# Hybrid decoder block on one core: projection and channel-mixing tiles multiplied in two halves of 256 tokens

## The chip, the core and the metric

The kernel runs on one core of one Trainium2 chip, as one program. A core has a matrix engine (TensorE, PE in the rows; its weight loads are listed as PEld), a vector engine (VectorE, DVE), a scalar engine (ScalarE, ACT), a general engine (GpSimd, POOL) and a queue engine (SyncE, SP), each with its own instruction stream, run in order. They wait for each other through semaphores. Data lies in SBUF, matmul results in the 8 banks of PSUM (512 float32 per partition each). The metric is the device time of one execution in microseconds, from runs without the profiler; one further execution is profiled.

## What is computed

One decoder block on 512 tokens of width 1024, all in float32:

```
mod = silu(c) @ w_ada + b_ada;  shift_m, scale_m, gate_m, shift_f, scale_f, gate_f = split(mod, 6)
h = modulate(rms_norm(x, g_pre_mix), shift_m, scale_m);  p = h @ w_in
y_a = rwkv7_mix(token-shifted part of p: r, k, v, decay, rate, gate) @ w_a     # 12 heads of 64
y_b = dilated_attention_mix(q, k, v of p) @ w_b                                # 3 groups of 4 heads
merged = sigmoid(p_ga) * y_a + sigmoid(p_gb) * y_b
x = x + gate_m * rms_norm(merged @ w_out, g_post_mix)
h = modulate(rms_norm(x, g_pre_ffn), shift_f, scale_f);  u, g = split(h @ w_ffn_in, 2)
out = x + gate_f * rms_norm((silu(u) * g) @ w_ffn_out, g_post_ffn)             # width 2816
```

## The kernel before

Every large product is made from three matmuls. A float32 operand is split into a high part, rounded to the type float32r, and a low part, the rest (`split`: ACT copies the high part, line 111, DVE subtracts for the low part, line 112). `mm3` then adds high x high, high x low and low x high into one PSUM bank. All matmuls of the kernel but the transposes are issued on line 108, so a line alone doesn't tell them apart; the tile names do.

A projection tile is 128 output channels by 512 tokens. Its weights, 128 x 1024, come in by one DMA on SP's queue into `raw` (three buffers), and are split into `hi` and `lo` (two buffers each). The moving operands are the normalised tokens: `hh`/`hl` for the input projection (`gemm_in`, 8 blocks of 128 input channels, so 24 matmuls), `zh`/`zl` for the output projection of the RWKV branch (`wa_tile`, 6 blocks, 18 matmuls), `h2h`/`h2l` for the channel mixing (`ffn_mm`, 24 matmuls). Three PSUM banks named `mm` hold these results; ACT and DVE read a bank once its last matmul is done.

The order of work: the normalisation of x with the first six input tiles (a code of its own, lines 340 on), then the RWKV part in two groups of three head pairs, then attention, the branch outputs and their merge, the product with w_out, and the channel mixing (22 pairs of tiles, then the product with w_ffn_out). The first four channel-mixing tiles are already multiplied in two halves of 256 tokens, because the second half of their input comes later.

An RWKV group is a chain through all engines. DVE substitutes the inverses of 32 x 32 blocks in 31 steps (`fP`, `fT`), transposes them into `T1` (line 529; `T` in the rows) and `N` (lines 530 and 531), PE multiplies `T1` with `Sg`, DVE and ACT copy the result to `Q`, PE multiplies `Q` with `N`, and then come 8 steps of a recurrence with small matmuls of 64 columns (`UV`, `H`, `xs`). The other input tiles, the list `SEQ`, are fillers that PE works on between the steps of this chain. Between them stand the key norms (`key_norm`, matmuls of 2 columns on `cs` and `t`, evacuated by DVE into `ssq`), the transposes of v (line 249) and the ada steps of DVE (line 163, `aw`).

A scheduler sets the order on each engine ahead of time. It takes the instructions in the order of the code, moved by priorities that count instructions: a group is issued with the priority of 1665 instructions earlier (`PRI`), the weights of a tile with a high priority, ada steps with 6681 (`APRI`). It keeps a time of its own for each instruction, and puts a filler where the chain is not ready by that time. On the chip an engine runs what stands next and waits for it.

Of the kernel before, what the change touches and what calls it, by code (L numbers as in the profile page):

```python
# [16 lines left out]
DRAM = bass.MemoryType.DRAM  # L17

P = 128
D = 1024  # L20
S = 512
KT = D // P
# [7 lines left out]
NF = DFF // P  # L30
KAPPA = math.exp(-0.5)
# [4 lines left out]
# columns of the packed per-channel vectors  # L36
# [9 lines left out]
# columns of the packed constants  # L46
# [12 lines left out]
# tiles of the packed weights  # L59
# [5 lines left out]
W_FI = 58  # L65
# [4 lines left out]
# order of the projection tiles around the two head groups  # L70
# [14 lines left out]
def block_kernel(ctx, tc, x, vec, cst, cst2, cst3, crow, ada, win0, lora, wts, wa, out):  # L85
# [41 lines left out]
    def mm3(o, wh, wl, ah, al, start, stop):  # L127
        mm(o, wh, ah, start, False)
        mm(o, wh, al, False, False)
        mm(o, wl, ah, False, stop)  # L130

# [44 lines left out]
    # DRAM scratch  # L176
# [28 lines left out]
    def gemm_in(i):  # L205
        wh, wl = weights(i)
        ps = bank("mm")
        for k in range(KT):
            w = slice(k * P, (k + 1) * P)
            mm3(ps, wh[:, w], wl[:, w], hh[:, k, :], hl[:, k, :], k == 0, k == KT - 1)  # L210
        return ps
# [51 lines left out]
    with ExitStack() as ph0:  # L263
# [82 lines left out]
        # LoRA hidden states  # L346
# [46 lines left out]
    def rwkv_group(gi):  # L393
        p0i = gi * GP
        # LoRA up weights: each of w2 and a2 with its high and low parts stacked on partitions
# [18 lines left out]
        for p in range(GP):  # L414
            pi = p0i + p
            cols = slice(p * P, (p + 1) * P)
            sgm = rp.tile([P, 2, NCH, 2 * C], F32, tag="Sg", name=nm("Sg"), bufs=3)
            Sg[p] = sgm
            scr.append(sgm.rearrange("p e c t -> p (e c t)"))
            # decay and in-context learning rate  # L420
            ps = bank(BT[gi][1])
            mm(ps, uw[:, cols], lw_h, True, False)
            mm(ps, uw[lo64, cols], lw_l[lo64], False, True)
            sg = scr[p][:, 0:520]
            sgv = sg.rearrange("p (c t) -> p c t", t=65)
            G.memset(sgv[:, :, 0:1], 0.0)
            A.activation(sgv[:, :, 1:65], ps.rearrange("p (c t) -> p c t", t=64), AF.Sigmoid, bias=vcol(V_W0, pi))
            ps = bank(BT[gi][2])
            mm(ps, ua[:, cols], la_h, True, False)
            mm(ps, ua[hi64, cols], lw_l[hi64], False, True)  # L430
            A.activation(scr[p][:, 1040:1552], ps, AF.Sigmoid, bias=vcol(V_A0, pi))
        for p in range(GP):
# [15 lines left out]
            # normalised key direction  # L448
# [23 lines left out]
            # gram blocks, keys first  # L472
# [21 lines left out]
        for p in range(GP):  # L494
# [6 lines left out]
            # v with tokens on partitions  # L501
# [7 lines left out]
        # inverses of the 32x32 diagonal blocks by substitution, one block per partition  # L509
# [44 lines left out]
        # chunk recurrence, the pairs of the group in step  # L554
# [5 lines left out]
        for c in range(NCH):  # L560
# [32 lines left out]
            if c % 2 == 1:  # L593
# [11 lines left out]
                # centre each head and sum the squares  # L605
# [16 lines left out]
        # group norm over each head, then back to channels on partitions  # L622
# [176 lines left out]
    def wa_tile(ct):  # L799
# [4 lines left out]
        for k in range(6):  # L804
            w = slice(k * P, (k + 1) * P)
            mm3(ps, wh[:, w], wl[:, w], zh[:, k, :], zl[:, k, :], k == 0, k == 5)
# [136 lines left out]
    for i in range(2, NF):  # L943
        pu, pg = bank("mm"), bank("mm")
        ffn_mm(pu, weights(W_FI + 2 * i), slice(0, S))
        ffn_mm(pg, weights(W_FI + 2 * i + 1), slice(0, S))
# [101 lines left out]
```

## Time and profile before

| | us |
|---|---|
| median of 3 runs | 1030.13 |
| lowest and highest run | 1029.17, 1035.16 |
| span of the profiled execution | 1036.7 |
| PE busy in it | 1004.9 |
| DVE busy in it | 580.4 |
| ACT busy in it | 397.2 |

The profiled execution is 6.6 us above the median. A row of the timeline gives the start, the duration, the engine, the line, the operation, output<-inputs with buffer numbers left out, the shape of the weights and of the moving operand, and the count; a bracket at the end is the time that the engine stood still before it, and what ended that. Matmuls overlap: the distance between two starts is what one costs in a stream, and it is shorter than its duration. The granted clock is PE's, as a share of full speed; 0.50 is the lower of its two levels. A float32 matmul (not float32r) takes several passes, so the chip counts more matmuls than the program.

### The profile page before, as it was taken

To read this page: it belongs to the slowest core of one execution; us is meant where nothing else is said; L and a number is where in the kernel's file an instruction comes from. 1 tells how busy PE (TensorE), PEld (TensorE's weight loads), DVE (VectorE), ACT (ScalarE), POOL (GpSimd) and SP (SyncE) were. 2 spreads that over 40 slices of the span, in tenths; PEclk is the share of its full clock that TensorE was granted. 3 is DMA by queue.
4 is the path that set the end of the run, shared out by engine and by line. 5 is a ranking of instruction groups with operands and counts; after the bars stand their busy time and mean duration, and the time that the engine had idled before them with its cause. 6 is when DMAs were issued, how large, how long until landed. Compare 5 with 4: busy or idle time off the path is not lost.

```text
span 1036.7 us, 13831 instructions
## 1 busy us (share of the span) xinstructions
PE 1004.9 (97%) x5468; PEld 787.8 (76%) x5468; DVE 580.4 (56%) x1050; ACT 397.2 (38%) x633; POOL 42.0 (4%) x85
## 2 busy tenths in 40 slices
PE   6999899999999999999999999999999999999997
PEld 4877778766777877677788768888888888888885
DVE  7885999643499984346646576763333333222134
ACT  7667453421366322331265234632323223222122
POOL 0000000100000010001000100010000000000000
PEclk9999999896999988999999999999999999999999
DMA  9743536322233222117525864063342332322322
GB/s 369 267 160 102 183 102 196 110 64 90 65 104 112 92 92 82 32 41 228 176 74 186 322 202 164 2 229 99 98 122 81 102 96 88 102 92 92 101 82 82
DMA packets 47170, 131.73 MB, mean 127 GB/s; under 512 B 11249, under 2 KB 12033, under 8 KB 47106
## 3 DMA queue, kind: packets, MB, share of 16 engines
q1 hardware_dynamic: 27792, 96.74, 28.7%
q10 hardware_dynamic: 13970, 16.27, 4.9%
q0 software_dynamic: 5344, 17.84, 4.8%
q8 instruction: 43, 0.70, 0.3%
q14 instruction: 21, 0.17, 0.1%
HBM read 116.14 MB, written 14.69 MB: 126 GB/s over the span
## 4 chain that ended last, share of the span: by engine, by line
PE 75%; DVE 11%; issue 7%; DMA 5%; ACT 1%; POOL 0%; ACTq 0%; SPq 0%; DVEq 0%; POOLq 0%
PE ps L108 73%; DVE lo L112 2%; DVE fP L521 1%; DVE fT L525 1%; DMA aw<-in_ada_dram 1%; DMA d_ya<-t 1%; DVE Sg L481 1%; DVE aw L163 1%; DMA gb<-d_gate 1%; DMA x<-in_x_dram 1%; DMA k<-d_k 1%; DMA t<-d_gate 1%; ACT xg L485 0%; PE ps L303 0%; PE ps L906 0%
## 5 line engine op out<-in xcount | busy, mean ns | idle before, releaser
L111 ACT CAST hi<-raw 128x1024 fp32r<-128x1024 f32 (+1 forms) x130 | 132.9, 1023 | 382.9 <-PE ps L108 329.3
L112 DVE TENSOR_TENSOR lo<-raw,hi 128x1024 fp32r<-128x1024 f32 (+1 forms) x130 | 154.6, 1190 | 185.5 <-ACT hi L111 179.7
L108 PE MATMUL ps<-hh,lo 128*128 128x512 f32 x432 | 179.1, 415 | 0.2 <-DVE lo L112 0.2
L108 PE MATMUL ps<-hl,hi 128*128 128x512 f32 x432 | 179.1, 415 | 0.0
L108 PE MATMUL ps<-hh,hi 128*128 128x512 f32 x432 | 175.7, 416 | 1.1 <-ACT hi L111 0.7
L108 PE MATMUL ps<-h2h,hi 128*128 128x512 f32 (+1 forms) x352 | 135.2, 386 | 0.7 <-ACT u L936 0.7
L108 PE MATMUL ps<-h2l,hi 128*128 128x512 f32 (+1 forms) x352 | 135.0, 385 | 0.0
L108 PE MATMUL ps<-h2h,lo 128*128 128x512 f32 (+1 forms) x352 | 134.8, 384 | 0.0
L108 PEld LDWEIGHTS ps<-hh,hi 128*128 128x128 f32 x432 | 84.7, 196 | 20.4 <-issue 2.1
L108 PEld LDWEIGHTS ps<-hh,lo 128*128 128x128 f32 x432 | 84.3, 195 | 19.1 <-issue 1.0
L108 PEld LDWEIGHTS ps<-hl,hi 128*128 128x128 f32 x432 | 84.5, 196 | 18.0 <-issue 0.8
L108 PEld LDWEIGHTS ps<-h2h,hi 128*128 128x128 f32 x352 | 65.8, 187 | 16.0 <-ACT u L936 0.9
L108 PEld LDWEIGHTS ps<-h2l,hi 128*128 128x128 f32 x352 | 65.9, 187 | 14.9
L108 PEld LDWEIGHTS ps<-h2h,lo 128*128 128x128 f32 x352 | 65.9, 187 | 14.8
L163 DVE SCALAR_TENSOR_TENSOR aw<-aw,silur 128x1024 f32<-128x1024 f32 x48 | 58.3, 1220 | 7.8 <-DMA aw<-in_ada_dram 7.7
L937 DVE TENSOR_TENSOR u<-u,ps 128x512 f32<-128x512 f32 x22 | 15.0, 687 | 70.2 <-PE ps L108 62.8
L108 PE MATMUL ps<-hi,fh 128*128 128x512 f32 x144 | 45.2, 394 | 0.0
L108 PE MATMUL ps<-hi,fl 128*128 128x512 f32 x144 | 45.2, 394 | 0.0
L108 PE MATMUL ps<-lo,fh 128*128 128x512 f32 x144 | 45.1, 394 | 0.0
L108 PE MATMUL ps<-UV,Sg 128*64 128x64 f32 x384 | 41.1, 247 | 0.0
L108 PEld LDWEIGHTS ps<-UV,Sg 128*64 128x64 f32 x384 | 26.8, 146 | 11.0 <-issue 3.2
L108 PEld LDWEIGHTS ps<-hi,fl 128*128 128x128 f32 x144 | 26.9, 187 | 6.7
(292 smaller groups left out, 1436.2 us busy)
## 6 DMA issues: line engine op xcount, KB each, us to landing
raw<-in_wts_dram SPq DMA_DIRECT2D x124, 512.0 KB, 3.6
aw<-in_ada_dram SPq DMA_DIRECT2D x40, 512.0 KB, 4.0
d_gate<-t POOLq DMA_DIRECT2D x16, 256.0 KB, 3.0
aw<-in_ada_dram POOLq DMA_DIRECT2D x8, 512.0 KB, 4.6
raw<-in_win_dram SPq DMA_DIRECT2D x8, 384.0 KB, 7.1
raw<-in_wa_dram SPq DMA_DIRECT2D x8, 384.0 KB, 3.8
x<-in_x_dram SPq DMA_DIRECT2D x4, 512.0 KB, 5.1
t<-d_gate ACTq DMA_DIRECT2D x8, 256.0 KB, 4.3
```

Source lines behind the costliest of these rows:

```text
L108: return nc.tensor.matmul(o, l, r, start=start, stop=stop)
L111: A.copy(hi, src)
L112: V.tensor_tensor(out=lo, in0=src, in1=r32(hi), op=ALU.subtract)
L163: V.scalar_tensor_tensor(out=aw, in0=aw, scalar=1.0, in1=silur, op0=ALU.mult, op1=ALU.mult, accum_out=modv[:, i:i + 1])
L481: V.tensor_tensor(out=sgm[:, e, c0:c0 + 4, :], in0=pgr[e].rearrange("p (c t) -> p c t", c=4), in1=m_gram[:, None, :].to_broadcast([P, 4, 2 ...
L521: V.tensor_tensor(out=pv, in0=fU[:, t + 1 + a:t + 1 + b, t, None].to_broadcast([P, b - a, m]), in1=fT[:, t, None, 0:m].to_broadcast([P, b ...
L525: V.tensor_tensor(out=rows, in0=rows, in1=pv, op=ALU.add)
L937: V.tensor_tensor(out=u, in0=u, in1=pg, op=ALU.mult)
```

## The change

`gemm_in`, `wa_tile` and the channel mixing from its third pair of tiles on (`i` from 2) go over a tile twice. First all blocks of input channels are multiplied for tokens 0 to 255 into the first half of the bank, then again for tokens 256 to 511 into the second half. Each weight block is thus loaded twice, and each matmul of 512 columns becomes two of 256. The program has 4576 matmuls before and 6832 after. The loads of weights, the splits, the banks and what reads them are the same, and SP's queue issues the same loads in the same order. In the channel mixing both tiles' weights are now asked for before the first tile's matmuls. The rest of the difference between the files is comments taken out, which moves the lines by one (up to line 205: `mm` stands on line 109) or more.

```diff
+HALVES = (slice(0, S // 2), slice(S // 2, S))
 ...
 def gemm_in(i):
     wh, wl = weights(i)
     ps = bank("mm")
-    for k in range(KT):
-        w = slice(k * P, (k + 1) * P)
-        mm3(ps, wh[:, w], wl[:, w], hh[:, k, :], hl[:, k, :], k == 0, k == KT - 1)
+    for t in HALVES:
+        for k in range(KT):
+            w = slice(k * P, (k + 1) * P)
+            mm3(ps[:, t], wh[:, w], wl[:, w], hh[:, k, t], hl[:, k, t], k == 0, k == KT - 1)
     return ps
 ...
 # wa_tile
-    for k in range(6):
-        w = slice(k * P, (k + 1) * P)
-        mm3(ps, wh[:, w], wl[:, w], zh[:, k, :], zl[:, k, :], k == 0, k == 5)
+    for t in HALVES:
+        for k in range(6):
+            w = slice(k * P, (k + 1) * P)
+            mm3(ps[:, t], wh[:, w], wl[:, w], zh[:, k, t], zl[:, k, t], k == 0, k == 5)
 ...
 # channel mixing, i from 2
-    ffn_mm(pu, weights(W_FI + 2 * i), slice(0, S))
-    ffn_mm(pg, weights(W_FI + 2 * i + 1), slice(0, S))
+    for ps, w in ((pu, weights(W_FI + 2 * i)), (pg, weights(W_FI + 2 * i + 1))):
+        for t in HALVES:
+            ffn_mm(ps, w, t)
```

The scheduler's order changes with it around the RWKV chain. On PE, where group 0's first inverse blocks are multiplied (`T_195`, output on `ps`), this stood before. The rows on `hh` and `hl` are fillers, the last matmuls of tile `ps_2212` and the first of `ps_2246`, which holds v of head pair 3:

```order
L108 MATMUL ps_2212<-hl,hi_2208 128x512
L108 MATMUL ps_2212<-hh,lo_2209 128x512
L108 MATMUL ps_2246<-hh,hi_2242 128x512
L108 MATMUL ps_2246<-hl,hi_2242 128x512
L108 MATMUL ps_2246<-hh,lo_2243 128x512
L108 MATMUL ps_2246<-hh,hi_2242 128x512
L108 MATMUL ps_1266<-T_195_1258,Sg_873 32x32 x8
L108 MATMUL ps_2246<-hl,hi_2242 128x512
L108 MATMUL ps_2246<-hh,lo_2243 128x512
L108 MATMUL ps_2246<-hh,hi_2242 128x512
L108 MATMUL ps_2246<-hl,hi_2242 128x512
L108 MATMUL ps_1266<-T_195_1258,Sg_873 32x32 x8
```

And now; `ps_2620` is the tile of gate 8, which stands one before v of pair 3 in `SEQ`, and the matmul of 2 columns is a key norm's:

```order
L109 MATMUL ps_2620<-hh,hi_2616 128x256
L109 MATMUL ps_1434<-T_195_1426,Sg_1041 32x32 x8
L109 MATMUL ps_2620<-hl,hi_2616 128x256
L109 MATMUL ps_2620<-hh,lo_2617 128x256
L109 MATMUL ps_2620<-hh,hi_2616 128x256
L109 MATMUL ps_2620<-hl,hi_2616 128x256
L109 MATMUL ps_2589<-cs_67,t_2587 128x2 x4
L109 MATMUL ps_2620<-hh,lo_2617 128x256
L109 MATMUL ps_2620<-hh,hi_2616 128x256
L109 MATMUL ps_2620<-hl,hi_2616 128x256
L109 MATMUL ps_2620<-hh,lo_2617 128x256
L109 MATMUL ps_1434<-T_195_1426,Sg_1041 32x32 x8
```

The first `T_195` matmuls have moved ahead by the columns of 0.90 tile, and ahead of three key norms of four program matmuls each. On DVE, at the same place, the end of the substitution, the transposes and the first copy stood like this (`ssq` evacuates a key norm):

```order
L387 TENSOR_SCALAR ssq_2178<-ps_2181 128x8
L521 TENSOR_TENSOR fP_1136<-fU_1134,fT_1135 128x87
L387 TENSOR_SCALAR ssq_2178<-ps_2189 128x8
L525 TENSOR_TENSOR fT_1135<-fT_1135,fP_1136 128x3x29
L387 TENSOR_SCALAR ssq_2178<-ps_2197 128x8
L521 TENSOR_TENSOR fP_1136<-fU_1134,fT_1135 128x60
L525 TENSOR_TENSOR fT_1135<-fT_1135,fP_1136 128x2x30
L521 TENSOR_TENSOR fP_1136<-fU_1134,fT_1135 128x31
L525 TENSOR_TENSOR fT_1135<-fT_1135,fP_1136 128x31
L529 STREAM_TRANSPOSE T_195_1258<-fT_1135 32x1024 x2
L163 SCALAR_TENSOR_TENSOR aw_2342,modv<-aw_2342,silur 128x1024
L530 STREAM_TRANSPOSE N_1259<-fT_1135 128x1024
```

And now (`lo_2675` is the low part of v of pair 3, which stood 12 rows ahead of the transposes before):

```order
L527 TENSOR_TENSOR fT_1303<-fT_1303,fP_1304 128x3x29
L523 TENSOR_TENSOR fP_1304<-fU_1302,fT_1303 128x60
L527 TENSOR_TENSOR fT_1303<-fT_1303,fP_1304 128x2x30
L523 TENSOR_TENSOR fP_1304<-fU_1302,fT_1303 128x31
L527 TENSOR_TENSOR fT_1303<-fT_1303,fP_1304 128x31
L531 STREAM_TRANSPOSE T_195_1426<-fT_1303 32x1024 x2
L532 STREAM_TRANSPOSE N_1427<-fT_1303 128x1024
L533 STREAM_TRANSPOSE N_1427<-fT_1303 128x1024
L544 COPY Q_1451<-ps_1434 32x256
L113 TENSOR_TENSOR lo_2675<-raw_2672,hi_2674 128x1024
L554 COPY N_1427<-ps_1456 32x32x8
L389 TENSOR_SCALAR ssq_2586<-ps_2589 128x8
```

The key norms, the split and one ada step have moved behind the transposes. On ACT two loads of an activation table, for the key norm's square root and for the sigmoid after it, have moved from ahead of the copy to `Q` into the recurrence's first step. In group 1 the first matmuls on `T_473` stand behind the columns of 40.90 tiles instead of 41.17, and the four transposes of v that stood ahead of them (line 249) now stand behind; the other differences are of a few fillers.

## Rows read from the trace of the kernel before

**Rows 1.** The page: the span, PE's busy time, and the granted clock in 40 slices.

```profile
span 1036.7 us, 13831 instructions
...
PE 1004.9 (97%) x5468; PEld 787.8 (76%) x5468; DVE 580.4 (56%) x1050; ACT 397.2 (38%) x633; POOL 42.0 (4%) x85
...
PEclk9999999896999988999999999999999999999999
```

**Rows 2.** Windows, channel mixing; columns: PE, PEld, DVE, ACT, POOL, clock, DMA, GB/s.

```profile
684.00:906.00 222.00, 222.00 (x954) 178.17 (x953) 82.97 (x97) 62.60 (x80) 3.76 (x7) 1.00 0.36 113
```

**Rows 3.** Timeline of PE, channel mixing: first and last of 53 starts.

```profile
799.73 0.39 PE L108 MATMUL ps<-h2l,hi 128*128 128x512 f32 x1
...
811.86 0.39 PE L108 MATMUL ps<-h2h,lo 128*128 128x512 f32 x1
```

**Rows 4.** Timeline of PE, output projection: first and last of 21 starts.

```profile
596.24 0.40 PE L108 MATMUL ps<-zh,lo 128*128 128x512 f32 x1
...
600.90 0.40 PE L108 MATMUL ps<-zl,hi 128*128 128x512 f32 x1
```

**Rows 5.** Timeline of PE, input projection: first and last of 22 starts.

```profile
479.80 0.39 PE L108 MATMUL ps<-hh,lo 128*128 128x512 f32 x1
...
484.56 0.39 PE L108 MATMUL ps<-hh,lo 128*128 128x512 f32 x1
```

**Rows 6.** Timeline of PE, first channel-mixing tiles in halves: first and last of 20 starts.

```profile
679.27 0.28 PE L108 MATMUL ps<-h2l,hx 128*128 128x256 f32 x1
...
681.42 0.28 PE L108 MATMUL ps<-h2h,lx 128*128 128x256 f32 x1
```

**Rows 7.** Timeline of PE, where these halves begin: first and last of 7 starts.

```profile
655.84 0.28 PE L108 MATMUL ps<-h2h,hi 128*128 128x256 f32 x1
...
656.54 0.28 PE L108 MATMUL ps<-h2h,hi 128*128 128x256 f32 x1
```

**Rows 8.** Timeline of PE, input projection at half clock: first and last of three starts.

```profile
202.41 0.63 PE L108 MATMUL ps<-hh,hi 128*128 128x512 f32 x1
...
203.26 0.63 PE L108 MATMUL ps<-hh,lo 128*128 128x512 f32 x1
```

**Rows 9.** Timeline of DVE around group 0's transposes into T and N.

```profile
178.85 1.22 DVE L112 TENSOR_TENSOR lo<-raw,hi 128x1024 fp32r<-128x1024 f32 x1
...
180.49 0.16 DVE L387 TENSOR_SCALAR ssq<-ps 128x8 f32<-128x8 f32 x1
...
182.84 0.17 DVE L387 TENSOR_SCALAR ssq<-ps 128x8 f32<-128x8 f32 x1 [1.70 <-PE ps L108]
...
183.88 4.02 DVE L529 STREAM_TRANSPOSE T<-fT 32x1024 f32<-32x1024 f32 x2
187.93 1.23 DVE L163 SCALAR_TENSOR_TENSOR aw<-aw,silur 128x1024 f32<-128x1024 f32 x1
...
191.48 0.43 DVE L542 COPY Q<-ps 32x256 f32<-32x256 f32 x1
```

**Rows 10.** Timeline of PE there: the last key norm, what follows it, and T.

```profile
181.85 0.95 PE L108 MATMUL ps<-cs,t 128*128 128x2 f32 x8
182.66 0.48 PE L108 MATMUL ps<-hh,lo 128*128 128x512 f32 x1
...
185.97 1.07 PE L108 MATMUL ps<-T,Sg 32*32 32x32 f32 x16 [0.53 <-DVE T L529]
```

**Rows 11.** Timeline of ACT there: a load of an activation table.

```profile
180.01 1.28 ACT L389 ACT_TABLE_LOAD   x1
```

**Rows 12.** Timeline of PE, group 1: the transposes of v, and T.

```profile
372.59 0.60 PE L249 MATMUL ps<-cs,t 128*128 128x128 f32 x4
374.95 1.07 PE L108 MATMUL ps<-T,Sg 32*32 32x32 f32 x16 [0.83 <-DVE T L529]
```

**Rows 13.** Timeline of PE, before attention: a wait for a DMA.

```profile
487.35 2.22 PE L108 MATMUL ps<-k,q 64*128 64x128 f32 x6 [2.40 <-DMA k<-d_k]
```

**Rows 14.** Windows right behind that wait (columns as in group 2).

```profile
487.60:494.50 6.90, 6.90 (x18) 4.99 (x18) 2.49 (x4) 0.00 (x0) 0.00 (x0) 0.51 0.73 225
```

**Rows 15.** Windows in group 0's recurrence (columns as in group 2).

```profile
211.00:238.00 27.00, 27.00 (x227) 18.41 (x225) 10.62 (x22) 7.43 (x17) 0.00 (x0) 1.00 0.26 79
238.00:255.00 17.00, 17.00 (x84) 11.01 (x84) 6.09 (x12) 4.05 (x9) 0.00 (x0) 0.51 0.19 63
```

**Rows 16.** The core's span and its mean granted clock.

```profile
core 0: 1036.7 us, clock 0.967
```

## The prediction

> **What bounds the kernel now.** I read the page first. TensorE (PE) is busy 1004.9 of 1036.7 us, and its granted clock is at or near full in nearly every slice, with dips in slices 8, 10, 15 and 16 [rows 1]. So the reader should expect the time to be PE's own work plus the few stretches in which PE stands still or runs at half clock; another engine matters only where PE waits for it. The windows show this for the channel mixing: from 684 to 906 us PE is busy 222.00 of 222.00 us at a granted clock of 1.00 [rows 2].
>
> Busy time does not price a matmul, because matmuls overlap: what counts is the distance from start to start, which the timeline gives. In the channel mixing, 52 steps of 512 columns lie between 799.73 and 811.86 us: 12.13 / 52 = 233.3 ns each [rows 3]. In the RWKV branch's output projection, 20 steps take 4.66 us, 233.0 ns [rows 4]. In the input projection, 21 steps take 4.76 us, 226.7 ns [rows 5]. The kernel already holds halves of 256 columns, in the first four channel-mixing tiles: 19 steps between 679.27 and 681.42 us are 113.2 ns each [rows 6], and just after that stretch begins 6 steps take 0.70 us, 116.7 ns each [rows 7]. Two halves are therefore 226.4 ns when the stream has settled and 233.3 ns when it has not.
>
> **The change, part by part.** *The matmuls.* 48 input projection tiles (24 matmuls each), 8 output projection tiles (18 each) and 40 channel-mixing tiles (24 each) are split: 1152 + 144 + 960 = 2256 matmuls become pairs, so 2256 matmuls and as many weight loads are added. The columns stay the same.
> - Channel mixing: same source tiles h2h and h2l, same kind of weights and same line as the halves of rows 6. 960 x (226.4 - 233.3) = -6.6 us.
> - Output projection: 144 x (226.4 - 233.0) = -1.0 us, taking the halves' price from rows 6.
> - Input projection: 1152 x (226.4 - 226.7) = -0.3 us; I take 0, because nothing shows halves of hh.
>
> That is -7.6 us. Bounds: if the halves keep the unsettled 116.7 ns, the pair costs 233.3, the first two parts gain nothing and the input projection loses 1152 x 6.6 = 7.6 us. From below, matmuls of 512 columns at half clock step by 0.85 / 2 = 425 ns [rows 8], so 256 columns at full clock cannot go below about 106 ns; then the pair is 213 ns and the three parts are worth 2256 x 13.7 + 1104 x 6.6 = 38 us. Rows 6 are near neither end; I take them.
>
> A rule speaks against this part. The Trainium skill, page "TensorE: Matmul & The Clock Gate", section "Back-to-back issue gap", gives N / 2.4 + 2.5 ns at full clock, a fixed part per matmul: an estimate from it is 2 x 109.2 = 218.3 ns for the pair against 215.8, so +5.6 us over 2256 pairs in place of -7.6. The rows differ from it: 233.3 and 226.7 for 512 columns and 113.2 for 256 grow with the columns, and no fixed part shows once the stream has settled.
>
> *The order.* A scheduler places the instructions, and twice as many matmuls shift what it puts between the steps of the RWKV chain. Counted in the two orders, group 0's first matmul on T stands behind 24.17 projection tiles before and 23.27 after: 0.90 tile, 21.6 matmuls x 0.2267 = 4.9 us of PE work less in front of it. Three key-norm groups move behind it too; one takes from 181.85 to 182.66 us, 0.8 us, so 2.4 us. PE comes to T 7.3 us of work earlier. VectorE (DVE) makes T, and comes earlier by less: it loses one split (1.1 us), three small ssq copies (0.3 us) and the wait of 1.70 us for the last of them [rows 9], 3.1 us. Before, PE waited 0.53 us there [rows 10]. The new stop is 7.3 - 3.1 = 4.2 us more, and it costs, since the filler that used to cover it is then run later by a PE that has no other free time. Behind the waiting T stand all fillers of the queue; ScalarE (ACT) and DVE wait for those to evacuate. Bounds: 0, if DVE's own wait was longer than the trace names, and 7.3.
>
> Next on that chain is Q. DVE needs 7.6 us from the start of T to Q, 6.4 without the 1.2 us ada step that also moves away, and 0.4 for Q itself [rows 9], 6.8; PE has T twice (1.0 us each), 7.5 full widths of filler (1.7) and two key-norm groups (1.6) after starting 2.1 us into T, 7.4 in all. So no wait: 0, at most 1. Two table loads of 1.28 us on ACT [rows 11] move from ahead of Q into the first step of the recurrence, where the chain's copies queue behind them; the fillers there cover most: +0.5, between 0 and 2.6.
>
> Group 1: T stands behind 41.17 tiles before and 40.90 after, 6.5 matmuls = 1.5 us, and four transposes, 0.4 us of a 0.60 us group; DVE's work ahead of T is unchanged. PE already waits 0.83 us there [rows 12], so all of it shows: +1.9, between 0 and 2.1. The other hops of both recurrences keep about as many columns between them; I take 0 (bounds -2 and +2). In the channel mixing and after it the order of DVE, ACT and the DMA queues is such that PE never waits before [rows 2]; a PE 3% faster leaves that so, and the cover is large (ACT and DVE are busy under half).
>
> *The clock.* Before 487.35 us PE waited 2.40 us for a DMA, and the next 6.9 us were granted 0.51, the 1.2 GHz level [rows 13, 14]. A new stop of some 4 us at T should do the same. The price: from 238 to 255 us at 0.51 PE started 84 matmuls, 4.9 per us; from 211 to 238 at 1.00, 227, 8.4 per us [rows 15]. A microsecond at half clock loses 0.41. I take 5 us more of it: +2.0. Bounds: both long stretches there (10 and 17 us) gone, -11; 30 us more, +12.
>
> Sum: -7.6 + 4.2 + 0.5 + 1.9 + 2.0 = +1.0 us on a profiled span of 1036.7, 1037.7. The median of the runs shown is 1030.1, 6.6 below the profiled one; I move the same step there: **1031 us**.
>
> **The rivals.**
> - *Only the gain.* The halves give 7.6 us and the stop at T doesn't show, because DVE in truth ran behind PE's fillers all along and now runs ahead. For it: DVE's 1.70 us wait for PE just there [rows 9]. Against: DVE is otherwise gapless in the stretch. 1030.1 - 7.6 = 1022.5.
> - *The clock falls for longer (slower).* The place is group 0's T to the end of its recurrence: less filler per step leaves PE at 1.2 GHz through pieces that had full clock [rows 15]. 30 us more at half clock cost 12.3 in place of 2.0: 1041.4. It decides the sign beyond 1% from about 27 us.
> - *A fixed cost per matmul (slower).* The halves stay at 116.7 ns [rows 7]: in place of -7.6 comes +7.6, 1046. For it: the fillers are often broken up. Against: rows 6. The skill's rule above has such a cost, smaller: an estimate from it is 13.2 us above my forecast, 1044.
> - *The halves are cheaper still.* In the input projection they come near the 106 ns bound: 1152 x 13.7 = 15.8 us less, 1015. For it only that 226.7 is above the bound.
>
> **How the numbers follow.** Chances: my forecast 0.52 (its own range 1024 to 1039), only the gain 0.16, the clock 0.13, the fixed cost 0.12, cheaper still 0.07. About 1% is what a measurement of this kernel can tell from no change: 1019.8 to 1040.4. Faster by more: 0.07 from the last, 0.04 from the low side of the second, 0.01 of the first, 0.12. Slower: 0.11 from the fixed cost, 0.08 from the clock, 0.03 from the first, 0.22. Same: 0.66. The range 1017 to 1043 leaves out most of the last and of the fixed cost and a part of the clock's, 0.19.
>
> **What would show it.** In the profile after: steps of 113 ns in the channel mixing and a stretch from its first full tile to the output matmuls shorter by some 6 us; steps of 113 ns in the input projection (116 or more: the fixed cost; under 110: cheaper); PE idle some 4 us ahead of group 0's first matmul on T and some 2 to 3 us ahead of group 1's, both for DVE; the time at half clock, now 2 x (1 - 0.967) x 1036.7 = 68 us by the mean granted clock [rows 16], some 5 us larger. I am wrong if T finds PE still busy, or if the recurrence's granted clock moves by much more than that.

## The result, and the profile after

The changed kernel takes 1070.8 us (median of 4 runs, 1066.4 to 1078.3), the kernel before 1032.6 in the same comparison. The ratio is 1.037 (95% interval 1.032 to 1.042): slower by 38 us, where I had forecast no change that can be measured and a range up to 1043. The profiled execution spans 1070.1 us in place of 1036.7. The ratios here and below leave out runs that took over 1.5% longer than the fastest of the same kernel.

The page of the kernel after, its span, busy times and the granted clock by slice (compare [rows 1]):

```profile
span 1070.1 us, 18345 instructions
...
PE 1027.1 (96%) x7724; PEld 925.9 (87%) x7724; DVE 581.5 (54%) x1050; ACT 396.9 (37%) x633; POOL 41.9 (4%) x85
...
PEclk9998999589989996999899999999999999999999
```

PE is still busy nearly throughout, DVE and ACT do what they did. The mean granted clock fell from 0.967 [rows 16] to 0.952:

```profile
core 0: 1070.1 us, clock 0.952
```

Twice the missing part times the span is the time at the half level: 68 us before, 2 x 0.048 x 1070.1 = 103 us now.

Windows by stage show where. The stages are cut at the same matmuls in both kernels: group 0's first on T, its first on UV, its first on lg_h (behind the recurrence), group 1's first on lw_h, its first on T. Columns: time, busy PE, PEld, DVE, ACT, POOL, granted clock, DMA share, GB/s. Before:

```profile
0.00:185.97 185.97, 172.40 (x826) 135.98 (x826) 154.74 (x345) 107.24 (x154) 7.05 (x20) 0.98 0.56 195
185.97:205.56 19.59, 19.59 (x225) 15.89 (x225) 12.32 (x16) 9.15 (x15) 3.55 (x5) 0.88 0.39 122
205.56:273.33 67.77, 67.77 (x512) 45.52 (x510) 25.43 (x54) 19.11 (x44) 0.54 (x1) 0.83 0.21 67
273.33:295.65 22.32, 22.32 (x118) 17.58 (x118) 16.09 (x26) 6.91 (x12) 3.16 (x9) 1.00 0.40 131
295.65:374.95 79.30, 74.50 (x403) 56.98 (x401) 76.02 (x202) 43.83 (x65) 4.30 (x8) 1.00 0.30 98
```

And after:

```profile
0.00:188.40 188.40, 170.11 (x1195) 152.06 (x1195) 153.45 (x341) 103.86 (x149) 7.05 (x20) 0.98 0.55 190
188.40:214.08 25.68, 25.68 (x257) 24.15 (x258) 9.37 (x14) 7.91 (x14) 3.01 (x4) 0.52 0.10 26
214.08:279.70 65.62, 65.62 (x601) 54.03 (x599) 25.77 (x54) 20.97 (x46) 0.54 (x1) 0.88 0.21 67
279.70:314.48 34.78, 31.76 (x254) 30.08 (x253) 21.50 (x33) 10.84 (x16) 4.24 (x11) 1.00 0.50 163
314.48:396.80 82.32, 77.48 (x603) 69.28 (x603) 75.69 (x200) 41.67 (x62) 3.23 (x6) 0.94 0.26 90
```

The time alone misleads, because a stage that leaves tiles undone hands them on. The lag of the changed kernel is the difference in time plus the projection tiles that it has done less by then (counted in the trace), at 24 x 0.2267 = 5.44 us each:

| point | before, us | after, us | tiles before | tiles after | lag, us |
|---|---|---|---|---|---|
| group 0, T | 185.97 | 188.40 | 24.17 | 23.27 | 7.3 |
| group 0, UV | 205.56 | 214.08 | 25.50 | 24.12 | 16.0 |
| group 0, lg_h | 273.33 | 279.70 | 29.12 | 27.58 | 14.8 |
| group 1, T | 374.95 | 396.80 | 41.17 | 40.90 | 23.3 |
| attention, first matmul | 487.35 | 516.48 | 49.4 | 49.3 | 29.7 |
| channel mixing begins | 655.84 | 686.50 | 54 | 54 | 30.7 |
| product with w_ffn_out begins | 906.59 | 939.89 | 54 | 54 | 33.3 |

Each column is one execution, and the start of group 0's T alone lay between 184.34 and 188.56 us in the kernels run below that keep the old order, so a lag is good to some microseconds only. Nearly half of the loss is there by group 0's UV, and 30 of 33 us before attention. Between lg_h and group 1's T another 8.5 us come in; PE stops there for 3.02 us for `uw`, an operand of the next group. From T to UV the clock fell from 0.88 to 0.52: 2 x 0.48 x 25.68 = 24.7 us at the half level in place of 4.7.

At T the timeline of PE shows the stop that I had forecast, with 3.00 us in place of 0.53 [rows 10]:

```profile
185.12 0.28 PE L109 MATMUL ps<-hh,hi 128*128 128x256 f32 x1
188.40 1.07 PE L109 MATMUL ps<-T,Sg 32*32 32x32 f32 x16 [3.00 <-DVE T L531]
```

And the matmuls. In the input projection, first and last of 22 starts, 2.52 / 21 = 120.0 ns per half, 240.0 per pair, in place of 226.7 [rows 5]:

```profile
59.77 0.28 PE L109 MATMUL ps<-hh,lo 128*128 128x256 f32 x1
...
62.29 0.28 PE L109 MATMUL ps<-hh,lo 128*128 128x256 f32 x1
```

In the channel mixing 22 starts are 2.38 / 21 = 113.3 ns each at 760 us, and later 2.47 / 21 = 117.6 (117.8 by the starts before rounding); in between stands the small matmul of modv, and from it on all halves keep the slower step:

```profile
759.70 0.28 PE L109 MATMUL ps<-h2h,lo 128*128 128x256 f32 x1
...
762.08 0.28 PE L109 MATMUL ps<-h2h,lo 128*128 128x256 f32 x1
...
792.79 0.27 PE L171 MATMUL ps<-cs,modv 128*8 128x128 f32 x1
...
819.88 0.28 PE L109 MATMUL ps<-h2l,hi 128*128 128x256 f32 x1
...
822.35 0.28 PE L109 MATMUL ps<-h2l,hi 128*128 128x256 f32 x1
```

### The profile page after: what moved, and what is told of

The parts are those of the page before. It is cut to its first block, busy times and chain, and to the rows that moved or that the text cites. A ratio compares the mean times of both kernels' runs of the same rounds, so it can differ in the third digit from the quotient of the medians.

```text
span 1070.1 us, 18345 instructions
## 1 busy us (share of the span) xinstructions
PE 1027.1 (96%) x7724; PEld 925.9 (87%) x7724; DVE 581.5 (54%) x1050; ACT 396.9 (37%) x633; POOL 41.9 (4%) x85
## 4 chain that ended last, share of the span: by engine, by line
PE 71%; DVE 11%; issue 8%; DMA 7%; ACT 2%; POOL 1%; ACTq 0%; SPq 0%; DVEq 0%; POOLq 0%
PE ps L109 69%; DMA aw<-in_ada_dram 4%; DVE lo L113 2%; DVE fP L523 2%; DVE fT L527 1%; DVE aw L164 1%; DMA d_ya<-t 1%; ACT xg L487 1%; DMA x<-in_x_dram 1%; DVE Sg L483 1%; PE ps L305 1%; DMA ya<-d_ya 1%; DMA gb<-d_gate 1%; DMA raw<-in_lora_dram 1%; DMA k<-d_k 0%
## 5 line engine op out<-in xcount | busy, mean ns | idle before, releaser
L109 PE MATMUL ps<-hh,lo 128*128 128x256 f32 (+1 forms) x816 | 249.8, 306 | 1.2 <-DVE lo L113 1.2
L109 PE MATMUL ps<-hl,hi 128*128 128x256 f32 (+1 forms) x816 | 249.3, 305 | 0.0
L109 PE MATMUL ps<-hh,hi 128*128 128x256 f32 (+1 forms) x816 | 245.6, 306 | 0.0
L109 PE MATMUL ps<-h2h,lo 128*128 128x256 f32 x672 | 187.6, 280 | 2.4 <-DVE lo L113 2.3
L109 PE MATMUL ps<-h2h,hi 128*128 128x256 f32 x672 | 187.9, 280 | 0.7 <-ACT u L939 0.7
L109 PE MATMUL ps<-h2l,hi 128*128 128x256 f32 x672 | 187.6, 280 | 0.1
L109 PEld LDWEIGHTS ps<-hh,lo 128*128 128x128 f32 x816 | 165.0, 202 | 7.4 <-issue 1.9
L109 PEld LDWEIGHTS ps<-hl,hi 128*128 128x128 f32 x816 | 165.3, 203 | 4.8 <-issue 1.0
L109 PEld LDWEIGHTS ps<-hh,hi 128*128 128x128 f32 x816 | 165.5, 203 | 4.4 <-issue 0.3
L109 PEld LDWEIGHTS ps<-h2h,hi 128*128 128x128 f32 x672 | 127.8, 190 | 1.4 <-ACT u L939 0.9
L109 PE MATMUL ps<-zh,hi 128*128 128x256 f32 (+1 forms) x112 | 33.4, 298 | 1.3 <-ACT hi L112 1.3
```

Of the source, the lines that this page charges most:

```text
L109: return nc.tensor.matmul(o, l, r, start=start, stop=stop)
```

## The experiments

Ratios are to the kernel before in the same comparison; that kernel's median was 1034.6 to 1035.8 us there.

### Which part of the change costs

**e_in** and **e_ffn** make one part of the change each: `gemm_in` alone, and the loop of the channel mixing alone.

> The halves in the input projection alone. From the trace after: 1152 pairs at 240.0 in place of 226.7 ns are 15.4 us, longer stops of PE ahead of the chains some 7 us, and more time at half clock some 10 us: about 1060 to 1066 us, ratio 1.030. The rival, that the slower halves alone count and the order costs nothing here: 1048, ratio 1.015.

Measured: 1065.5 us, 1.030 (1.025 to 1.036).

> The halves in the channel mixing alone. From the trace after: 3 us longer (a stop of 2.3 us on a weight tile, and halves at 113.3 ns up to the small matmul of modv and 117.8 behind it): 1033 to 1036 us, ratio 1.003. My prediction's term: 6.6 us shorter, ratio 0.994. If the 117.8 belongs to a state that the stream falls into by chance, the stretch may lie at either.

Measured: 1037.6 us, 1.0015 (0.998 to 1.005). So the input projection carries 3.0 of the 3.7%; the channel mixing shows neither gain nor loss clear of noise, its halves again first at 113.3 ns and then, behind a wait of 0.32 us for a weight tile at 699 us, at 117.8. The output projection's 8 tiles were not run alone.

### What sets the step of a matmul

**series** puts series of matmuls behind the last product.

```
+ bw = weights(W_FI)
+ for n, mo, wo, po in SERIES:              # width, first column of fh/fl, of hi/lo, of the bank
+     ps = bank("mm")
+     mm(ps[:, 0:8], bw[0][:, 0:128], fhf[:, 0:8], True, True)
+     for k in range(7):
+         w, t = slice(k * P + wo, k * P + wo + P), slice(k * S + mo, k * S + mo + n)
+         mm3(ps[:, po:po + n], bw[0][:, w], bw[1][:, w], fhf[:, t], flf[:, t], k == 0, k == 6)
```

> The kernel before with two rounds of 19 series of 21 matmuls behind its last product (each in the order of mm3, on fh and fl, with one matmul of 8 columns ahead of it). The series differ in the width, in the first column of the moving operand, of the weights, and of the bank. In the kernel all large operands begin 32 bytes behind a multiple of 64; a first column of 8 puts an operand on the multiple, 1008 puts fh at the same place modulo 4096 bytes as the weights. Theory A, the start address: a matmul costs 6.67 ns for each 64 bytes that its operand touches in a partition, so 512 columns cost one such step less from column 8 (about 220 to 227 ns in place of 227 to 233) and 256 columns 113 or less in place of 113 to 120. Theory B, the place of moving operand and weights to each other: 1008 with weights from 0, and 1016 with weights from 8, differ from the other pairs, 226.7 for 512 columns and 120 for 256 there, 233.3 and 113 to 118 elsewhere. Theory C, a fixed cost per matmul: 128 columns 67 ns, 256 columns 120, 384 columns 173, 512 columns 227, whatever the start. Theory D, the state in which a stream begins: the two rounds of one series differ.

Measured, steps near the end of a series: with moving operand and weights at the same place modulo 4096 bytes 226.7 ns for 512 columns and 120.0 for 256; at other places about 229 to 233 and 117 to 120. The absolute start changes nothing (0 with 0 and 8 with 8 read 228.9 both, and 117.8), the two rounds agree within a nanosecond or two. 384 columns take 173.3 and 128 columns 111.7, first and last of 20 starts:

```profile
1207.63 0.28 PE L112 MATMUL ps<-fl,hi 128*128 128x128 f32 x1
...
1209.75 0.27 PE L112 MATMUL ps<-fh,lo 128*128 128x128 f32 x1
```

So theory B stands, A and D fall, and C does for 128 columns, the narrowest that the series hold: no matmul of a series, each with a load of 128 x 128 weights, came under about 111 ns. The 106 ns that the half-clock step of [rows 8] leaves for a half of 256 columns lie below that, and no half reached them. The Trainium skill, page "TensorE: Matmul & The Clock Gate", section "LDWEIGHTS (loading the stationary operand)", gives P / 1.2 ns for a load, 106.7 for 128 columns; the 111.7 lies near it, but that the load is what holds the matmul no run shows.

**aligned_before** moves all large operands by 32 bytes in the kernel before.

```
- modv = const.tile([P, 48], F32, name="modv")
+ modv = const.tile([P, 56], F32, name="modv")      # and zl, h2l and dg likewise
```

> The kernel before, with whole tiles, but with every large matmul operand moved 32 bytes, so that it begins at a multiple of 64 (three tiles made 32 bytes longer; order of instructions the same). Theory A (6.67 ns per 64 bytes touched): 3408 matmuls of 512 columns lose one step, 226.7 to 220.0 in the input projection and 233.3 to 226.7 or 220 in the channel mixing and the products: some 15 to 30 us shorter, 1000 to 1015 us, while the last eight weight tiles of the product with w_ffn_out, which stay 32 bytes off, keep 233. Theories B to D: no change, 1030 us.

Measured: 1034.4 us, 0.9995 (0.997 to 1.003). Theory A is dead in the kernel too.

**distances** repeats series with `SERIES = [(n, (r - 64) // 4 % 1024, 0, 0) for n in (512, 256) for r in (0, 16, 32, ... 2048)]`.

> The kernel before with 32 series of 21 matmuls behind its last product, 512 and 256 columns at 16 distances (0 to 2048 bytes, modulo 4096) between the start of the moving operand and that of the weights. Theory of the distance: 512 columns 226.7 ns at 0 and up to 233.3 elsewhere, 256 columns 120 at 0, and at 192, the distance of the channel mixing, 113.3 or 117.8. If only the place within a weight block of 512 bytes counts, 512, 1024 and 2048 read as 0. Rival, that the rate belongs to the stretch or the buffer and the earlier series differed by accident: no pattern over the distances.

Measured, in ns:

| distance, bytes | 0, 256, 512, 1024, 2048 | 16 | 32 | 48 | 64, 320 | 96 | 128, 384 | 160 | 192, 448 |
|---|---|---|---|---|---|---|---|---|---|
| 512 columns | 226.7 | 231.7 | 233.3 | 233.3 | 228.9 | 233.3 | 232.4 | 234.3 | 233.3 |
| 256 columns | 120.0 | 118.7 | 117.8 | 118.3 | 117.8 | 120.0 | 118.7 | 118.7 | 113.3 |

The pattern repeats every 256 bytes. Timeline of PE, settled ends of series: 512 columns at distance 0 (7 steps, 1.59 us) and at 192 (15 steps, 3.50 us), 256 columns at 0 (9 steps, 1.08 us) and at 192 (13 steps, 1.47 us):

```profile
1023.93 0.39 PE L111 MATMUL ps<-fl,hi 128*128 128x512 f32 x1
...
1025.52 0.39 PE L111 MATMUL ps<-fh,lo 128*128 128x512 f32 x1
...
1061.97 0.39 PE L111 MATMUL ps<-fh,lo 128*128 128x512 f32 x1
...
1065.47 0.40 PE L111 MATMUL ps<-fh,lo 128*128 128x512 f32 x1
...
1101.71 0.28 PE L111 MATMUL ps<-fh,lo 128*128 128x256 f32 x1
...
1102.79 0.28 PE L111 MATMUL ps<-fh,lo 128*128 128x256 f32 x1
...
1121.93 0.28 PE L111 MATMUL ps<-fh,hi 128*128 128x256 f32 x1
...
1123.40 0.28 PE L111 MATMUL ps<-fl,hi 128*128 128x256 f32 x1
```

hh and hl lie at distance 0 from the weights, zh, zl, h2h and h2l at 192. Distance 0 is the best place for whole tiles and among the worst for halves; 192 is the reverse. That is why whole tiles read 226.7 in the one and 233.3 in the other [rows 3, 5], and why the price of a half, read at 192 [rows 6], was wrong for hh.

**in_shifted** is e_in with hh and hl moved to distance 192.

```
- hh = hp_.tile([P, KT, S], F32R, name="hh")
+ hh = hp_.tile([P, KT * S + 48], F32R, name="hh")[:, 48:].rearrange("p (k s) -> p k s", k=KT)
```

> The halves in the input projection alone, as e_in, with hh and hl moved by 192 bytes, the distance to the weights that h2h and h2l have in the channel mixing; order of instructions as in e_in. Theory of the distance: the halves leave 120.0 ns for 117.8 or 113.3, 1152 pairs x 4.4 to 13.3 ns: 5 to 15 us less than e_in, 1050 to 1060 us, and the key stops of PE and the time at half clock as in e_in. Rival (the rate belongs to the stretch): 1065 us.

Measured: 1069.3 us, 1.034 (1.029 to 1.039). The halves did go to 113.3 ns (21 steps in 2.38 us), and the kernel did not get faster:

```profile
149.78 0.28 PE L109 MATMUL ps<-hh,hi 128*128 128x256 f32 x1
...
152.16 0.28 PE L109 MATMUL ps<-hh,hi 128*128 128x256 f32 x1
```

Span and mean granted clock of in_shifted:

```profile
core 0: 1066.2 us, clock 0.946
```

So the slow halves, the nearest explanation of the loss, are not what bounds it: with them gone, PE stood still longer (span less busy time 46.6 us, 38.5 in e_in) and the clock was lower still (0.946, 0.952 in e_in). The rate expected of a distance was right; what I expected of the time fell.

### Which part of the order costs

The step of a matmul being no answer, the order was the next suspect. In every kernel so far that had 23.27 tiles ahead of group 0's T (the changed one, e_in, in_shifted) 3.0 to 3.7% were lost; no kernel with 24.17 lost any. **in_rec**, **in_rest**, **in_ahead0**, **in_ahead1**, **in_last** and **in_six** halve the input tiles of a part of the program only, by the number of the call:

```
+ ncall[0] += 1
- for t in HALVES:
+ for t in HALVES if ncall[0] < 18 else (slice(0, S),):      # in_ahead0; other conditions in the others
```

> Halves only in the 11 input tiles that are fillers from T to the last copy of the recurrence in both groups (the 19th to 24th and 36th to 40th call of gemm_in); 24.15 and 41.62 tiles stand ahead of the two T, 25.42 ahead of group 0's first UV matmul (before 24.17, 41.17, 25.50; after the change 23.27, 40.90, 24.12). Theory, the moved order costs the time, not the halves as such: PE's stop at T of 0.5 us, 5 to 11 us at half clock from T to the first UV matmul, ratio 1.00 to 1.005 (264 pairs at 240 are 3.5 us). Rival, the halves themselves in the chain let the clock fall: 20 us and more at half clock there and 1.015.

Measured: 1.000 (0.996 to 1.004).

> The reverse: halves in the other 37 input tiles, whole tiles as fillers of the recurrences; 23.27 and 40.90 tiles ahead of the two T and 24.12 ahead of the first UV matmul, as after the change. Theory, the moved order costs the time: a stop of 3 us at T, about 25 us at half clock from T to the first UV matmul, 1060 to 1066 us, ratio 1.025 to 1.03, nearly all of e_in. Rival (halves as fillers of the recurrences cost): 888 pairs at 240 are 11.8 us and the stop 2.5, ratio 1.014.

Measured: 1.027 (1.021 to 1.033). The windows from group 0's T to its first UV matmul, of in_rec and of in_rest:

```profile
186.95:207.78 20.83, 20.83 (x254) 19.55 (x254) 12.20 (x16) 9.13 (x15) 3.55 (x5) 0.82 0.35 115
```

```profile
185.53:211.22 25.69, 25.69 (x254) 23.64 (x254) 9.35 (x14) 7.91 (x14) 3.00 (x4) 0.50 0.09 26
```

With halves as fillers there and the order kept, the clock of the stretch, 0.82, lies among those of the kernels that keep the old order (0.74 to 0.92); with whole tiles there and the moved order it runs at the half level from end to end, and PE's stop at T is 3.0 us (0.6 in in_rec). The halves in the chain are harmless; the order ahead of it is not.

> Halves only in the 18 input tiles that run ahead of group 0's T (calls 1 to 18 of gemm_in): 23.27 tiles ahead of T and 24.12 ahead of the first UV matmul, as after the change; group 1 within 0.1 to 0.3 of a tile of before (41.25, 42.96). Theory, the place of group 0's T costs most: stop 3 us, 25 us at half clock from T to UV, ratio 1.015 to 1.025. Rival, the slower halves alone: 432 pairs at 240 in place of 226.7 ns are 5.8 us, ratio 1.006.

Measured: 1057.6 us, 1.024 (1.016 to 1.032). The same window:

```profile
189.05:214.78 25.73, 25.73 (x254) 23.67 (x255) 9.36 (x14) 7.91 (x14) 3.01 (x4) 0.50 0.09 25
```

Halving the 18 tiles ahead of group 0's T makes about two thirds of the 3.7%, though their 432 pairs cost 5.8 us at most (0.6%).

> Halves only in the 11 input tiles between group 0's recurrence and group 1's T (calls 25 to 35): group 0 as before, 40.69 tiles ahead of group 1's T in place of 41.17 (after the change 40.90), 41.79 ahead of its first UV matmul in place of 42.79. Theory, the moved order costs: about 0.5 tile (2.7 us) more of a stop or of work behind and 10 us more at half clock, ratio 1.006 to 1.010. Rival, the slower halves alone: 264 pairs, 3.5 us, 1.003.

Measured: 1.005 (1.002 to 1.008), which holds the rival's 1.003 as well as the lower end of the theory.

> Halves only in the last 8 input tiles (calls 41 to 48), behind the recurrences; order as before. This prices slow halves by themselves: 192 pairs at 240.0 in place of 226.7 ns are 2.6 us, ratio 1.0025, if PE sets the pace there, 1.000 if not.

Measured: 1.004 (1.000 to 1.008). The interval holds the 2.6 us that the step of 192 slow pairs says, and hardly excludes that they cost nothing.

> Halves only in calls 7 to 12 of gemm_in: 23.75 tiles ahead of group 0's T (0.42 less than before, and two groups of key norms less), but 1.29 tiles of filler from T to the first UV matmul, as before (1.33). Theory, too little filler lets the clock fall: 5 to 11 us at half clock from T to UV although PE stops some 2 to 4 us at T, ratio 1.002 to 1.006. Rival, the stop lets it fall: 20 us and more at half clock there, ratio 1.010 to 1.015.

Measured: 0.999 (0.994 to 1.004), which excludes the rival's price and leaves only the lowest end of the theory's. The ten runs spread from 1028 to 1057 us, with a median of 1042.5 for all ten. The stop that both theories build on did not come: PE went from the fillers to T without one, and the window from T to the first UV matmul is like that of the old order:

```profile
186.31:205.84 19.53, 19.53 (x225) 15.74 (x224) 10.93 (x17) 9.72 (x16) 3.55 (x5) 0.91 0.29 96
```

So it doesn't set stop against filler. It does show halves ahead of T, 0.42 tile less in front of it and no stop, without the fall of the clock.

The parts add up to 2.4 + 0.0 + 0.5 + 0.4%, 3.3 of e_in's 3.0.

### What lets the clock fall behind T

> The kernel before, whole tiles, with the transpose that makes T repeated by one and a third in group 0 (the same values written again), so that T comes 2.5 us later and PE's stop ahead of it grows from 0.5 to 3.0 us, as after the change; the same 24.17 tiles stand ahead of T, and the same fillers behind it within 0.1 of a tile on average. Theory, the stop lets the clock fall: from T to the first UV matmul 20 to 25 us at half clock (5 to 8 in the kernels with whole tiles so far) and the stretch some 6 us longer beyond the stop: ratio 1.008 to 1.010. Rival, it is the 0.5 tile less of filler in that stretch that does it: 5 to 8 us at half clock, ratio 1.002.

```
  for e in range(2):
      V.transpose(t1a[:, e], fT[64 * e:64 * e + 32].rearrange("k a b -> k b a"))
+     if gi == 0 and e == 1:
+         V.transpose(t1a[:, e], ...)            # once more
+         V.transpose(t1a[:, e, 0:10], ...)
```

Measured: 1.001 (0.998 to 1.004), and a miss. T's first matmuls need only the first transpose, so PE stopped 0.5 us at T as before and 1.3 us later; the question was not put.

**little_filler** has the repetition at `e == 0`.

> The kernel before, whole tiles, with the transpose that begins T in group 0 repeated by one and a third (2.5 us); 0.91 tile more stands ahead of T (25.08), so PE should not stop there at all, and only 0.38 tile of filler is left from T to the first UV matmul (before 1.33, after the change 0.85). Theory, too little filler between T and UV lets the clock fall: 20 us or more at half clock there although PE never stopped, the stretch as long as 19 us or more with 5 us less work in it, ratio 1.005. Rival, the stop does it: 5 to 11 us at half clock there and ratio 1.002.

Measured: 1.004 (1.000 to 1.008). The scheduler put the extra tile in front, with the DVE work that belongs to it; T came at 194.24 and PE stopped 2.6 us all the same. The stretch is at the half level throughout:

```profile
194.24:208.66 14.42, 14.42 (x201) 11.91 (x201) 7.83 (x12) 6.20 (x12) 3.00 (x4) 0.50 0.34 110
```

It has both suspects, the stop and little filler, so its mean clock does not tell them apart. All kernels in which PE stopped 2.6 us or more at T ran the stretch at 0.50 to 0.52; of those that stopped about 0.5 us or not at all none was below 0.74. But each of the former also had 0.38 to 0.85 tile of filler there in place of 1.27 to 1.33.

The order in time tells more. In in_rest PE stood still from 182.55 to 185.53 us, and the clock fell at 184.80, before T's first matmul and any filler behind it; in in_ahead0 it fell at 188.70, with T at 189.05. Here in_rest's stop up to the fall, the rest of the stop, and what follows T; in_ahead0's end of the stop; and the changed kernel, where the clock fell 0.8 us behind the start of T:

```profile
182.55:184.80 2.25, 0.01 (x1) 0.00 (x0) 2.08 (x6) 0.52 (x1) 0.54 (x1) 1.00 0.30 117
184.80:185.53 0.73, 0.00 (x0) 0.00 (x0) 0.70 (x2) 0.00 (x0) 0.00 (x0) 0.52 0.00 0
185.53:229.20 43.67, 43.67 (x355) 35.40 (x355) 13.67 (x23) 13.29 (x24) 3.54 (x5) 0.50 0.16 55
...
188.70:189.05 0.35, 0.00 (x0) 0.00 (x0) 0.32 (x2) 0.00 (x0) 0.00 (x0) 0.50 0.00 0
...
188.40:189.20 0.80, 0.80 (x15) 0.80 (x16) 0.80 (x1) 0.00 (x0) 0.00 (x0) 1.00 0.00 0
189.20:223.40 34.20, 34.20 (x308) 31.53 (x306) 11.61 (x21) 12.65 (x22) 3.55 (x5) 0.50 0.17 55
```

So the filler behind T can't have begun the fall; what stands ahead of it is the stop. The stop of 3.02 us for `uw` did the same in the changed kernel, with the half level from 315.50 us:

```profile
315.50:325.80 10.30, 10.30 (x26) 5.98 (x27) 6.47 (x11) 5.33 (x8) 0.00 (x0) 0.50 0.28 102
```

Not every such stop does it: behind the one of 2.32 us in the channel mixing of the changed kernel the clock stayed at 1.00. What sets how long the clock stays down, 34.2 us behind T and 10.3 behind `uw`, no run separates. In little_filler, with the least filler, it was up again at 214.50 us, 20.3 us behind T.

Nor is a stretch at half clock a loss by itself. Little_filler's took 14.42 us with 0.95 tile less filler in it, 5.17 us at full clock; together that is the 19.59 us of the kernel before.

### A faster version

**placed** and **placed_all** take the kernel before and move the operands of all large products to distance 0, where whole tiles step by 226.7 ns.

```
- modv = const.tile([P, 48], F32, name="modv")
+ modv = const.tile([P, 64], F32, name="modv")      # 64 bytes more; modf lies in it now
- modf = xp.tile([P, 16], F32, name="modf")
+ modf = modv[:, 48:64]
- h2l = h2p.tile([P, KT, S], F32R, name="h2l")      # and zl
+ h2l = h2p.tile([P, KT * S + 32], F32R, name="h2l")[:, 0:KT * S].rearrange("p (k s) -> p k s", k=KT)
```

> The kernel before, whole tiles and order as before, with zh, zl, h2h, h2l, mh, ml, fh and fl moved to distance 0 from the weights (modulo 4096 bytes), as hh and hl have. Theory of the distance: 226.7 in place of 233.3 ns for 960 matmuls of the channel mixing, 192 of the RWKV branch's and the other branch's products, 432 of the product with w_ffn_out and 96 of that with w_out, 11.2 us less, and 1.3 us more for the 192 halves of the first four channel-mixing tiles (113.3 to 120): some 10 us less, ratio 0.990. Rival (the rate belongs to the stretch): 1.000.

Measured: 1026.4 us, 0.992 (0.988 to 0.995).

> As placed, with the last eight weight tiles of the product with w_ffn_out and the last six or so of that with w_out at distance 0 modulo 256 bytes too (two tiles of padding). 192 more matmuls at 226.7 in place of 233.3 ns: 1.3 us less than placed, ratio 0.990 to the kernel before, 0.955 to the kernel after the change.

Measured: 1025.0 us, 0.990 (0.987 to 0.993); the two intervals overlap, so the 1.3 us more are not shown. In placed, 56 starts of the channel mixing are 12.47 / 55 = 226.7 ns apart, in place of 233.3 [rows 3]:

```profile
799.72 0.39 PE L109 MATMUL ps<-h2l,hi 128*128 128x512 f32 x1
...
812.19 0.39 PE L109 MATMUL ps<-h2h,lo 128*128 128x512 f32 x1
```

What the change was to win by halves, some 7 us, whole tiles win by a little padding: the gain lies where PE sets the pace, and the order is not touched.

## Why the prediction was wrong

**What bounds the kernel.** I said that PE's own work sets the time. From the channel mixing on that holds: there placed took 246.0 us in place of 250.8 up to the product with w_ffn_out and 127.3 in place of 130.1 behind, and its steps say 5.1 and 2.9 us less. In the RWKV part it does not: in_shifted took 13 ns from each of 1152 pairs and won nothing. There PE's rate, the place of the fillers and the clock make up one balance, and what one gives back another takes.

**Input projection, 0 us.** The step that failed first: "I take 0, because nothing shows halves of hh." The price of rows 6 belongs to another pair of places; the halves took 120.0 ns, 1152 x 13.3 = 15.3 us by the sum, and my upper bound of 116.7 did not hold them. That "no fixed part shows" is true at distance 192 alone of the places measured; at distance 0 a pair of halves costs 13.3 ns more than the whole tile's matmul. The sign that I had set for the rival of a fixed cost, 116 ns or more in the input projection, came. That hh and h2h differ already as whole tiles, 226.7 and 233.3 [rows 3, 5], was the warning, and I read it only as a term to subtract from. The runs show as well that this is not what bounds the result (in_shifted).

**Channel mixing, -6.6 us; output projection, -1.0.** The halves reached 113.3 ns but left them for good at 792.79 us, for 117.8. The stretch is 253.4 us in place of 250.8, 2.3 of it a new wait for a weight tile: the matmuls as such gained nothing. The Trainium skill, page "TensorE: Matmul & The Clock Gate", section "Back-to-back issue gap", had spoken against a gain, and none came, but its 109.2 ns for 256 columns was reached by no series here (113.3 to 120.0). In the output projection they stayed at 113 to 114 ns, so that term held.

**The stop at T.** Place, cause and sign held: 3.00 in place of 0.53 us, +2.5 where I had +4.2. The two arrivals that I worked it out from can't be checked one by one, since T began anywhere from 184.34 to 188.56 us in kernels with the old order; only their difference repeats, a stop of 0.5 us in each of them. Group 1's grew by 0.7, from 0.83 to 1.49, where I had +1.9. Two stops I did not see: 3.0 us for `uw` ahead of group 1, and the 2.3 us in the channel mixing. In all PE stood still for 43.0 us in place of 31.8 (span less busy time).

**The clock, +2.0 us.** The term that failed most. I took 5 us more at half clock, by the one wait of rows 13 and 14. It was 103 - 68 = 35 us, 14 us at my price of 0.41 us lost per microsecond, an estimate that no run checks; 20 of the 35 lie between T and UV, where PE ran at half clock for nearly all of the stretch. I had named this as a rival ("The clock falls for longer"), with 30 us, and gave it 0.13. Its size fits the whole program by luck. At the place it named, from T to the end of the recurrence, the time at half clock grew from 27.7 to 40.4 us, by 13, because the recurrence itself ran at 0.88 in place of 0.83; most of the rest lies around group 1's T, which I had not named.

**The range.** With the measured terms my sum is 15.3 + 0.3 - 0.9 for the halves, 2.5 + 0.7 + 5.3 for the stops and 14.1 for the clock: +37 on 1036.7, against +33.4 measured, so they overlap by some 4 us. That the sum comes near is no proof of its terms: in_shifted took the first one away and the time stayed. But I had made rivals of two things that happen together: the slow halves gave 1046 alone, the clock 1041 alone, both by the same prices 1057, far beyond my range. They have one cause in common, the split, which brought the slow step and the moved order at once; rivals with a common cause don't share out the chance between them.

**What is shown and what not.** Shown: the loss comes with the halves in the tiles ahead of the chains, group 0's above all (in_ahead0, in_rest against in_rec and e_ffn), not with their step (in_shifted), and with it come the stop at T and the long fall of the clock, which begins in or right behind the stop. Argued: that the moved order carries it. No kernel of whole tiles had the order of the changed one, and little_filler, whole tiles with a stop of 2.6 us and half clock behind it, lost 0.4% only. Shown: the distance between moving operand and weights sets the step of an undisturbed stream, but for the two steps at distance 192. Not settled: how long the clock stays down, and what that costs.

## What to carry to other kernels

A matmul's price holds for the places of its two operands: take it from a run with these places, and where two streams of the same width differ by 3%, look at the distance between moving operand and weights before changing anything else. Where a scheduler places fillers between the steps of a chain, a change in the fillers' number of instructions can change the chain's order; count what stands ahead of each step before and after, and price what falls behind, the stop and the clock together, since they came together here. Where the chain sets the pace, faster fillers alone may win nothing, as in in_shifted.

## What was not expected of the hardware

- The step of back-to-back matmuls depends on the distance between the start of the moving operand and of the weights, with a period of 256 bytes: 226.7 to 234.3 ns for 512 columns, 113.3 to 120.0 for 256. Distance 0 is the best place for 512 and among the worst for 256; 192 is the best for 256 and among the worse for 512. The Trainium skill, page "TensorE: Matmul & The Clock Gate", section "Step-by-step: what each phase is for", says that loading the next weights takes no read bandwidth from the running matmul; the series measured differ by place alone, so the two operands are not independent here.
- Matmuls of 128 columns with a load of 128 x 128 weights each step by 111.7 ns, hardly less than 256 columns at the best place (113.3).
- At distance 192 a stream of halves has two lasting steps, 113.3 and 117.8 ns, and changes between them at a break. In the changed kernel one small matmul in between took it to 117.8 for the rest of the 147 us, and a stop of 2.32 us at 733 us had brought it from 117.8 back to 113.3; in e_ffn a wait of 0.32 us took it to 117.8.
- The same order of instructions spread by more than 1% between executions, with the share of time at half clock: the kernel before took 1026.4 us at a mean granted clock of 0.983 and 1040.2 at 0.970. That limits the comparisons here.
- A stop of PE of 2.6 to 3.4 us at T was followed by 20 to 44 us at the half level (little_filler, in_rest), and in in_rest and in_ahead0 the clock fell 0.7 and 0.35 us before PE started again.
